# A third seven-product column set, block sums by accumulating transfers and four shared block buffers, in a decoder trunk on one core

## The chip, the core and the metric

The kernel runs on one NeuronCore of a Trainium2 chip. The metric is the device time of one execution in microseconds (us). A profile is one execution recorded instruction by instruction; engine names are those of the profile: PE (TensorE, matmuls; PEld is its weight load), DVE (VectorE), ACT (ScalarE), POOL (GpSimd), SP (SyncE, which issues most transfers).

## The reference, cut to what matters

Four layers on 256 rows of width 1024. Each layer is a half-step SwiGLU feed-forward network (FFN), a token mixer with memory attention, and another half-step FFN; every part is normalised before and after. So there are eight FFNs, and they hold most of the multiplications.

```python
def swiglu_ffn(x, w_gate_up, w_down):
    gate, up = jnp.split(x @ w_gate_up, 2, axis=-1)
    return (jax.nn.silu(gate) * up) @ w_down
...
x = x + 0.5 * rms_norm(swiglu_ffn(rms_norm(x, g[0]), ffn_w_gate_up[i, 0], ffn_w_down[i, 0]), g[1])
```

`w_gate_up` is 1024 x 5632 (gate and up of width 2816 each), `w_down` 2816 x 1024. All is float32.

## The kernel before, in words

**A product in three matmuls.** Each float32 operand is split into a high part `hi` (rounded to the fp32r type by ACT, L309) and the rest `lo` (DVE, L310), and a product is hi·hi + hi·lo + lo·hi (`mm3`, L334 to L336). So each unit of weights (128 partitions x 1024 columns, 512 KB) needs one ACT and one DVE operation before PE can use it.

**The ring of units.** `plan()` writes out the order in which PE takes units. `split_next` splits the next one into a ring of `RING` = 10 hi/lo pairs; `pump`, called from `slot` after each unit that PE has used, keeps the splits up to nine units ahead. Raw units come from HBM by SP's queue (`fetch`, L240) into three `raw` buffers.

**Column sets.** An FFN's 2816 gate and up columns are worked in six sets: sets 0 to 4 of 512 gate columns and the 512 up columns that go with them, set 5 of 256 and 256. For each set, the 256 rows (two halves, t = 0 and 1) are multiplied by gate and up, `silu` and the multiplication give T, T is transposed by PE (`turn_set`, L557) and split into `hh` and `hl`, and the rows of `w_down` that match (D units, 12 matmuls each, L684) are added into two accumulators. `FILL` says how many D units stand in which set; the last 8 stand at the end of the FFN.

**Normal sets and seven-product sets.** A normal set has 8 units and 96 matmuls (2 row halves x 8 chunks of the inner dimension x 3 parts x gate and up). In the sets of `SEVEN` (2 and 4) the product is seen as 2 x 2 blocks: row halves by inner halves of x, and inner halves by (gate, up) of the weights (b11, b12, b21, b22). Winograd's form of Strassen's method needs seven block products instead of eight: 14 units and 84 matmuls (`product`, L615). Its price is sums of blocks. Those of x are made once per FFN (`sums`, L599). Those of the weights are made in `operand`: for products 2, 3, 4 and 5 DVE adds one block to another before the split (L277; two halves each, so eight per set). Those of the results are made in `seven`: `snap` copies a PSUM buffer to SBUF (ACT, L623), and DVE adds (c11 L635, c22 L646, c12 L658).

In `seven`, three PSUM buffers a, b, c are taken at the start. Products 0, 3, 4 and 5 accumulate in a, 1 in b, 2 and 6 in c. There are four such buffers (`rot`), and the transposes of the set before, `turned(s - 1)`, stand after product 1 and take two. D units stand after product 3 (two) and product 4 (two).

**Block buffers.** The four weight blocks of a seven-product set are 8 KB per partition each. They borrow the buffers of tiles that are idle in an FFN: tags `rows` (normalised rows), `mgh` and `mgl` (memory and mixer outputs), and `q22` in the FFN's own pool. A block is loaded in two halves, in the order b11, b21, b12, b22, one half per call of `slot` in the set before.

**Order on the queues.** Each engine works its queue in order. The order is fixed when the program is built, from when operands and buffers are expected to be free; SP's transfers are thus often issued ahead of where they stand in the source, as soon as their buffer is released.

Of the kernel before, what the change touches and what calls it, by code (L numbers as in the profile page):

```python
# [53 lines left out]


SETS = 6
SEVEN = (2, 4)
FILL = {1: (2, 2), 3: (1, 1)}
QUADS = 8


def ffn_chunks(l, f):
    order = []
    nd = 0

    def fill(n):
        nonlocal nd, order
        order += [("D", l, f, nd + i) for i in range(n)]
        nd += n

    for s in range(SETS):
        if s in SEVEN:
            for ops, n in (((0, 1, 2, 3), 2), ((4,), 2), ((5, 6), 0)):
                order += [("S", l, f, s, op, h) for op in ops for h in range(2)]
                fill(n)
            continue
        for c, n in zip(("e",) if s == SETS - 1 else ("g", "u"), FILL.get(s, (0, 0))):
            order += [(c, l, f, s, i) for i in range(4)]
            fill(n)
    return order + [("D", l, f, j) for j in range(nd, NF)]  # L80
# [123 lines left out]
class Trunk:  # L204
    def __init__(self, ctx, tc, io):
        self.ctx, self.tc, self.nc, self.io = ctx, tc, tc.nc, io
        pool = lambda name, bufs=1, **kw: ctx.enter_context(tc.tile_pool(name=name, bufs=bufs, **kw))
        self.const = pool("const")
        self.wp = pool("wp")
        self.main = pool("main")  # L210
        self.small = pool("small", 4)
        self.ps = pool("ps", space=bass.MemoryType.PSUM)
        self.dram = pool("dram", space=bass.MemoryType.DRAM)
        self.plan = plan()
        self.offs = {}
# [11 lines left out]
        self.quad = None  # L227
        self.quad_loads = deque()

    def rot(self, *shape):  # L230
# [18 lines left out]
        self.raws.append((t, a * b))  # L249
        self.loaded += 1  # L250

    def new_quad(self, fp, l, f, s):
        self.quad = [None] * 4
        self.quad_pool = fp
        self.quad_set = (l, f, s)
        self.quad_loads = deque(quads(l, f, s))

    def load_quad(self):
        key = self.quad_loads.popleft()
        q, h = key[4:]  # L260
        if h == 0:
            pool, tag = ((self.main, "rows"), (self.main, "mgh"), (self.main, "mgl"), (self.quad_pool, "q22"))[q]
            self.quad[q] = pool.tile([P, 2, 1024], F32, tag=tag, name="quad")
        self.fetch(self.quad[q][:, h, :], key)

    def quads_for(self, key):
        if self.quad is None or self.quad_set != key[1:4]:
            return None
        return max(0, len(self.quad_loads) - (QUADS - (2 * min(key[4], 3) + key[5] + 1)))

    def can_split(self):
        key = self.plan[self.split_n]
        return key[0] != "S" or self.quads_for(key) == 0

    def operand(self, op, h):
        b11, b12, b21, b22 = (t if t is None else t[:, h, :] for t in self.quad)
        add = lambda x, y: self.nc.vector.tensor_tensor(out=x, in0=x, in1=y, op=ALU.add)  # L277
        if op == 2:
            add(b11, b12)
        elif op == 3:  # L280
            add(b11, b22)
        elif op == 4:
            add(b12, b22)
        elif op == 5:
            add(b21, b11)
        return (b11, b21, b11, b11, b12, b21, b22)[op]

    def split_next(self):
        key = self.plan[self.split_n]
        hi = self.wp.tile([P, 1024], F32R, tag="hi", name="hi", bufs=RING)  # L290
        lo = self.wp.tile([P, 1024], F32R, tag="lo", name="lo", bufs=RING)
        if key[0] == "S":
            for _ in range(self.quads_for(key)):
                self.load_quad()
            self.split(hi, lo, self.operand(*key[4:]))
# [60 lines left out]
    def ln_stages(self, st, t, ps, post_scale, post_eps, gpost, gpre):  # L356
# [9 lines left out]

        def rows():
            if st["rows"] is None:
                st["rows"] = self.main.tile([P, 2, D], F32, tag="rows", name="rows")
            return st["rows"][:, t, :]  # L370

        def s1():
# [30 lines left out]
                nc.scalar.activation(out=keep(t, k0 // 4), in_=ps, func=AF.Copy)  # L403

    def new_xt(self, a="xth", b="xtl"):
        return tuple(self.main.tile([P, KD, SEQ], F32R, tag=n, name=n) for n in (a, b))

    def boundary(self, ys, post, pre):
# [120 lines left out]
    def ffn(self, l, f, post_next, pre_next, last=False):  # L529
        nc, tc = self.nc, self.tc  # L530
        with tc.tile_pool(name=f"ffn{l}{f}", bufs=1, reuse_waits="tile") as fp:
# [61 lines left out]
            def sums():  # L593
# [10 lines left out]
                a11 = tuple(v[:, 0:4, 0:P] for v in xt)  # L604
                a12 = tuple(v[:, 4:8, 0:P] for v in xt)
                a22 = tuple(v[:, 4:8, P:] for v in xt)
                return a11, a12, S1, S2, S3, a22, S4

            def product(s, op, ps, fresh=False, after=None):
                for h in range(2):  # L610
# [15 lines left out]
            def seven(s):  # L626
                tt = nc.vector.tensor_tensor
                v = {}
                a, b, c = self.rot(), self.rot(), self.rot()
                T0, T1 = T[s]  # L630
                keep = lambda n: lambda: v.__setitem__(n, snap(a))
                product(s, 0, a, True, keep("P1"))

                def c11():
                    tt(out=v["P1"], in0=v["P1"], in1=b, op=ALU.add)  # L635
                    silu(T0, v["P1"])

                product(s, 1, b, True, c11)
                turned(s - 1)
                product(s, 2, c, True)  # L640
                product(s, 3, a, False, keep("U2"))
                fill(2)

                def c22():
                    v["U3"] = snap(a)
                    tt(out=v["U3"], in0=c, in1=v["U3"], op=ALU.subtract)  # L646

                product(s, 4, a, False, c22)
                fill(2)

                def c21():
                    silu(T1, a)
                    tt(out=T1, in0=T1, in1=v["U3"], op=ALU.mult)

                product(s, 5, a, False, c21)

                def c12():
                    tt(out=v["U2"], in0=c, in1=v["U2"], op=ALU.subtract)  # L658
                    tt(out=T0, in0=T0, in1=v["U2"], op=ALU.mult)

                product(s, 6, c, False, c12)

            first_set()
            left = sums()
# [36 lines left out]
            for s in range(1, SETS):  # L701
                T[s] = [tile_T(), tile_T()]
                if s + 1 in SEVEN:
                    self.new_quad(fp, l, f, s + 1)
# [59 lines left out]

    def mem_kv(self, l):
        nc = self.nc
        km = self.mp.tile([P, 2, SEQ], F32, name="km")
        vm = self.mp.tile([P, 2, SEQ], F32, name="vm")
        ps = self.rot().rearrange("p (a b) -> p a b", a=2)
        for c in range(2):  # L770
            self.cols_unit(ps[:, c, :], self.memg, self.take("K", l, c))
# [55 lines left out]
        return got[0]  # L827

    def q_mem(self, l, c0, xt):
        qm = self.mp.tile([P, 2, SEQ], F32, name="qm")  # L830
# [498 lines left out]
```

## Time and profile before

| | before |
|---|---|
| runs shown (3) | median 1902.22 us, 1894.52 to 1907.36 |
| the profiled execution | 1902.04 us, span 1900.2 us |
| granted TensorE clock | 0.999 of full speed |
| read from HBM | 359.95 MB, 190 GB/s over the span |
| the chain that ended last, by engine | PE 60%, DVE 17%, DMA 12%, ACT 5%, issue 4% |
| block sums on DVE (L277) | 128, 154.2 us |
| splits of blocks (L309 and L310) | 224 each, 232.7 us on ACT and 269.4 us on DVE |

The profile gives for each engine the time in which it was busy; for PE, instructions overlap, so that a busy PE can still be a PE that waits. In lists of groups a row is: line, engine, operation, output <- inputs by the program's tile names, shape, xcount | busy us in all, mean ns of one | idle us of the engine just before them, and what ended that idle time. In a timeline a row is: start in us, duration in us, engine and operation, count, and in brackets the idle time before it and its releaser. In lists of waits the numbers are us in total, times, and the longest. In lists of transfers the last number is the median time from issue to landing.

### The profile page before, as it was taken

To read this page: it belongs to the slowest core of one execution; us is meant where nothing else is said; L and a number is where in the kernel's file an instruction comes from. 1 tells how busy PE (TensorE), PEld (TensorE's weight loads), DVE (VectorE), ACT (ScalarE), POOL (GpSimd) and SP (SyncE) were. 2 spreads that over 40 slices of the span, in tenths; PEclk is the share of its full clock that TensorE was granted. 3 is DMA by queue.
4 is the path that set the end of the run, shared out by engine and by line. 5 is a ranking of instruction groups with operands and counts; after the bars stand their busy time and mean duration, and the time that the engine had idled before them with its cause. 6 is when DMAs were issued, how large, how long until landed. Compare 5 with 4: busy or idle time off the path is not lost.

```text
span 1900.2 us, 25015 instructions
## 1 busy us (share of the span) xinstructions
PE 1858.8 (98%) x9406; PEld 1550.4 (82%) x9406; DVE 1514.9 (80%) x1828; ACT 1085.9 (57%) x1469; POOL 59.8 (3%) x115
## 2 busy tenths in 40 slices
PE   7999999999999999999999999999999999999998
PEld 5888888787878897888888889888888878988886
DVE  6987888896879768889697966878877886878894
ACT  5655656564656545655565656555556555656562
POOL 0000100000000000000000000000000000100000
PEclk9999999999999999999999999999999999999999
DMA  8646747545663663754566357275476535747632
GB/s 295 235 167 200 233 156 266 205 140 176 233 222 115 199 203 111 266 198 145 180 231 233 112 185 238 102 246 184 151 229 227 189 127 183 243 156 244 220 105 86
DMA packets 103865, 362.65 MB, mean 191 GB/s; under 512 B 12084, under 2 KB 16576, under 8 KB 103616
## 3 DMA queue, kind: packets, MB, share of 16 engines
q1 hardware_dynamic: 103568, 359.47, 56.5%
q8 instruction: 74, 1.21, 0.3%
q0 software_dynamic: 176, 1.59, 0.2%
q14 instruction: 47, 0.39, 0.1%
HBM read 359.95 MB, written 1.06 MB: 190 GB/s over the span
## 4 chain that ended last, share of the span: by engine, by line
PE 60%; DVE 17%; DMA 12%; ACT 5%; issue 4%; POOL 1%; ACTq 0%; SPq 0%; DVEq 0%
PE acc L684 15%; DMA raw<-in_w 12%; PE rot L615 9%; PE rot L334 9%; PE rot L336 9%; PE rot L335 9%; DVE lo L310 9%; ACT hi L309 4%; DVE quad L277 3%; PE acc L944 3%; PE rot L557 1%; PE rot L399 1%; PE rot L848 1%; DVE x L378 1%; PE rot L880 1%
## 5 line engine op out<-in xcount | busy, mean ns | idle before, releaser
L310 DVE TENSOR_TENSOR lo<-raw,hi 128x1024 fp32r<-128x1024 f32 (+1 forms) x515 | 624.4, 1219 | 216.9 <-ACT hi L309 207.5
L309 ACT ACTIVATE hi<-raw 128x1024 fp32r<-128x1024 f32 (+1 forms) x515 | 542.1, 1055 | 397.0 <-DMA raw<-in_w 259.0
L334 PE MATMUL rot<-hi,xth 128*128 128x512 f32 (+3 forms) x1072 | 414.9, 387 | 2.5 <-ACT hi L309 1.6
L336 PE MATMUL rot<-hi,xtl 128*128 128x512 f32 (+3 forms) x1072 | 411.6, 384 | 1.2 <-DVE xtl L310 1.1
L335 PE MATMUL rot<-lo,xth 128*128 128x512 f32 (+3 forms) x1072 | 411.6, 384 | 0.0
L309 ACT ACTIVATE hi<-quad 128x1024 fp32r<-128x1024 f32 x224 | 232.7, 1056 | 156.5 <-DVE quad L277 83.4
L310 DVE TENSOR_TENSOR lo<-quad,hi 128x1024 fp32r<-128x1024 f32 x224 | 269.4, 1220 | 7.2 <-ACT hi L309 6.2
L334 PEld LDWEIGHTS rot<-hi,xth 128*128 128x128 f32 x1072 | 202.1, 189 | 41.4 <-ACT hi L309 2.1
L336 PEld LDWEIGHTS rot<-hi,xtl 128*128 128x128 f32 x1072 | 201.9, 188 | 41.3 <-DVE xtl L310 2.3
L335 PEld LDWEIGHTS rot<-lo,xth 128*128 128x128 f32 x1072 | 202.1, 189 | 38.2
L684 PE MATMUL acc<-lo,hh 128*128 128x512 f32 x640 | 198.9, 390 | 0.0
L684 PE MATMUL acc<-hi,hh 128*128 128x512 f32 x640 | 198.0, 390 | 0.0
L684 PE MATMUL acc<-hi,hl 128*128 128x512 f32 x640 | 197.2, 389 | 0.0
L277 DVE TENSOR_TENSOR quad<-quad 128x1024 f32<-128x1024 f32 x128 | 154.2, 1220 | 0.9
L684 PEld LDWEIGHTS acc<-hi,hl 128*128 128x128 f32 x640 | 120.1, 188 | 25.0 <-DVE hl L310 0.2
L684 PEld LDWEIGHTS acc<-lo,hh 128*128 128x128 f32 x640 | 120.2, 188 | 24.8
L684 PEld LDWEIGHTS acc<-hi,hh 128*128 128x128 f32 x640 | 119.5, 188 | 24.3
L615 PE MATMUL rot<-hi,sh 128*128 128x512 f32 x256 | 103.0, 402 | 6.8 <-DVE snap L635 6.8
L615 PE MATMUL rot<-lo,sh 128*128 128x512 f32 x256 | 100.0, 391 | 0.0
L615 PE MATMUL rot<-hi,sl 128*128 128x512 f32 x256 | 97.4, 390 | 0.0
L374 DVE TENSOR_TENSOR rows<-acc,gpost 128x1024 f32<-128x1024 f32 x24 | 29.3, 1222 | 74.9 <-ACT junk L373 74.8
L615 PE MATMUL rot<-hi,xtl 128*128 128x512 f32 x192 | 74.8, 389 | 0.0
(212 smaller groups left out, 2439.8 us busy)
## 6 DMA issues: line engine op xcount, KB each, us to landing
raw<-in_w SPq DMA_DIRECT2D x504, 512.0 KB, 4.3
quad<-in_w SPq DMA_DIRECT2D x128, 512.0 KB, 5.8
gpre<-in_norm_g SPq DMA_DIRECT2D x12, 512.0 KB, 5.1
gpost<-in_norm_g SPq DMA_DIRECT2D x12, 512.0 KB, 5.4
memraw<-in_mem_t SPq DMA_DIRECT2D x32, 128.0 KB, 3.2
raw<-in_w SPq DMA_DIRECT2D x8, 384.0 KB, 3.5
sw<-in_sw SPq DMA_DIRECT2D x2, 768.0 KB, 8.1
cb<-cd POOLq DMA_DIRECT2D x1, 1536.0 KB, 9.9
```

The costliest lines, as they stand in the source:

```text
L277: add = lambda x, y: self.nc.vector.tensor_tensor(out=x, in0=x, in1=y, op=ALU.add)
L309: self.nc.scalar.activation(out=hi, in_=src, func=AF.Copy)
L310: self.nc.vector.tensor_tensor(out=lo, in0=src, in1=hi.bitcast(F32), op=ALU.subtract)
L334: mm(out, a[0], b[0], start=start, stop=False)
L335: mm(out, a[0], b[1], start=False, stop=False)
L336: mm(out, a[1], b[0], start=False, stop=stop)
L374: nc.vector.tensor_tensor(out=rows(), in0=ps, in1=gpost, op=ALU.mult)
L378: nc.vector.scalar_tensor_tensor(out=x, in0=rows(), scalar=r, in1=x, op0=ALU.mult, op1=ALU.add)
L399: nc.tensor.transpose(ps[:, (k - k0) * P:(k - k0 + 1) * P], rows[:, k * P:(k + 1) * P], self.ident)
L615: nc.tensor.matmul(ps, a[i], w[j][:, kk, :], start=fresh and h == kk == i == j == 0, stop=h == kk == i == 1, skip_group_check=True)
L684: mm(ys[t][:, n * 512:(n + 1) * 512], x, y[:, 0, n * 512:(n + 1) * 512], start=(j == 0 and x is a[0] and y is w[0]), stop=(j == NF - 1 and ...
L944: self.nc.tensor.matmul(o["y"][t][:, h * 512:(h + 1) * 512], x, y[:, 0, h * 512:(h + 1) * 512], start=(j == 0 and x is a[0] and y is w[0]) ...
```

## The change

Sets 2, 3 and 4 now have seven products. The seven products are put in another order (the block sums are 11, 21, 11+12+22, 12+22, 11+12, 21+11+12+22, 22), so that two of the four weight sums are left to DVE (product 2's addition and product 4's subtraction, four operations per set with their halves), and two are done by transfers with accumulation issued on POOL's queue (`gather`): b22 into b12 as soon as both have landed, and the new b11 into b21 after product 2's sum. Product 2 and the later ones therefore need all four blocks of their set. In `seven`, c is taken after product 3; products 0, 2, 3 and 5 accumulate in a, 1 in b, 4 and 6 in c; D units stand after product 2 and after product 6 (`SFILL`: two and two in sets 2 and 4, one and one in set 3). The number of D units ahead of the end of the FFN, 14, is as before. The four block buffers become four buffers of one tag, `big`, shared by the blocks of all three sets, the normalised rows and the memory and mixer outputs. The small tiles km, vm and qm of the mixers move into the four `snap` buffers.

```diff
-SEVEN = (2, 4)
-FILL = {1: (2, 2), 3: (1, 1)}
-QUADS = 8
+SEVEN = (2, 3, 4)
+FILL = {1: (2, 2)}
+SFILL = {2: (2, 2), 3: (1, 1), 4: (2, 2)}
+SEVEN_OPS = ((0, 1, 2), (3, 4, 5, 6))
...
+    def big(self, *shape, dtype=F32):
+        return self.main.tile([P, *shape], dtype, tag="big", name="big", bufs=4)
...
         if h == 0:
-            pool, tag = ((self.main, "rows"), (self.main, "mgh"), (self.main, "mgl"), (self.quad_pool, "q22"))[q]
-            self.quad[q] = pool.tile([P, 2, 1024], F32, tag=tag, name="quad")
-        self.fetch(self.quad[q][:, h, :], key)
+            quad[q] = self.big(2, 1024)
+        self.fetch(quad[q][:, h, :], key)
+        if q == 3:
+            self.gather(quad[1][:, h, :], quad[3][:, h, :])
+
+    def gather(self, x, y):
+        self.nc.gpsimd.dma_start(out=x, in_=y, accum_op=ALU.add)
...
-        return max(0, len(self.quad_loads) - (QUADS - (2 * min(key[4], 3) + key[5] + 1)))
+        left = sum(k[1:4] == key[1:4] for k in self.quad_loads)
+        need = (2 * key[4] if key[4] < 2 else 6) + key[5] + 1
+        return max(0, need - (8 - left))
...
         if op == 2:
-            add(b11, b12)
-        elif op == 3:
-            add(b11, b22)
+            self.nc.vector.tensor_tensor(out=b11, in0=b11, in1=b12, op=ALU.add)
+            self.gather(b21, b11)
         elif op == 4:
-            add(b12, b22)
-        elif op == 5:
-            add(b21, b11)
-        return (b11, b21, b11, b11, b12, b21, b22)[op]
+            self.nc.vector.tensor_tensor(out=b11, in0=b11, in1=b22, op=ALU.subtract)
+        return (b11, b21, b11, b12, b11, b21, b22)[op]
...
-                return a11, a12, S1, S2, S3, a22, S4
+                return a11, a12, S2, S3, S1, a22, S4
...
-                a, b, c = self.rot(), self.rot(), self.rot()
+                a, b = self.rot(), self.rot()
...
                 product(s, 1, b, True, c11)
                 turned(s - 1)
-                product(s, 2, c, True)
-                product(s, 3, a, False, keep("U2"))
-                fill(2)
+                product(s, 2, a, False, keep("U2"))
+                fill(SFILL[s][0])
+                product(s, 3, a, False, keep("U3"))
+                c = self.rot()
 
                 def c22():
-                    v["U3"] = snap(a)
                     tt(out=v["U3"], in0=c, in1=v["U3"], op=ALU.subtract)
 
-                product(s, 4, a, False, c22)
-                fill(2)
+                product(s, 4, c, True, c22)
...
                 product(s, 6, c, False, c12)
+                fill(SFILL[s][1])
...
-        km = self.mp.tile([P, 2, SEQ], F32, name="km")
-        vm = self.mp.tile([P, 2, SEQ], F32, name="vm")
+        km = self.main.tile([P, 2, SEQ], F32, tag="snap", name="km", bufs=4)
+        vm = self.main.tile([P, 2, SEQ], F32, tag="snap", name="vm", bufs=4)
```

The tiles `rows` of a boundary and the pairs of `new_xt("mgh", "mgl")` are taken from `big` in the same way, and qm from `snap`.

More of the change, by code (lines that the diff above doesn't have):

```diff
@@ L72, in ffn_chunks @@
         if s in SEVEN:
-            for ops, n in (((0, 1, 2, 3), 2), ((4,), 2), ((5, 6), 0)):
+            for ops, n in zip(SEVEN_OPS, SFILL[s]):
                 order += [("S", l, f, s, op, h) for op in ops for h in range(2)]
@@ L226, in __init__ @@
         self.xf = {}
-        self.quad = None
+        self.quads = {}
         self.quad_loads = deque()
@@ L250, in load_next, with new_quad @@
         self.loaded += 1
[L252 to L256, printed above, removed]
+    def new_quad(self, l, f, s):
+        self.quads[l, f, s] = [None] * 4
+        self.quad_loads.extend(quads(l, f, s))
+    def big(self, *shape, dtype=F32):
+        return self.main.tile([P, *shape], dtype, tag="big", name="big", bufs=4)
     def load_quad(self):
         key = self.quad_loads.popleft()
+        quad = self.quads[key[1:4]]
         q, h = key[4:]
         if h == 0:
-            pool, tag = ((self.main, "rows"), (self.main, "mgh"), (self.main, "mgl"), (self.quad_pool, "q22"))[q]
-            self.quad[q] = pool.tile([P, 2, 1024], F32, tag=tag, name="quad")
-        self.fetch(self.quad[q][:, h, :], key)
+            quad[q] = self.big(2, 1024)
[4 more added lines that the diff above has]
+        self.nc.gpsimd.dma_start(out=x, in_=y, accum_op=ALU.add)
     def quads_for(self, key):
-        if self.quad is None or self.quad_set != key[1:4]:
+        if key[1:4] not in self.quads:
             return None
-        return max(0, len(self.quad_loads) - (QUADS - (2 * min(key[4], 3) + key[5] + 1)))
+        left = sum(k[1:4] == key[1:4] for k in self.quad_loads)
+        need = (2 * key[4] if key[4] < 2 else 6) + key[5] + 1
+        return max(0, need - (8 - left))
     def can_split(self):
@@ L273, in can_split, with operand @@
         return key[0] != "S" or self.quads_for(key) == 0
-    def operand(self, op, h):
-        b11, b12, b21, b22 = (t if t is None else t[:, h, :] for t in self.quad)
-        add = lambda x, y: self.nc.vector.tensor_tensor(out=x, in0=x, in1=y, op=ALU.add)
+    def operand(self, l, f, s, op, h):
+        b11, b12, b21, b22 = (t if t is None else t[:, h, :] for t in self.quads[l, f, s])
         if op == 2:
-            add(b11, b12)
-        elif op == 3:
-            add(b11, b22)
+            self.nc.vector.tensor_tensor(out=b11, in0=b11, in1=b12, op=ALU.add)
+            self.gather(b21, b11)
         elif op == 4:
-            add(b12, b22)
-        elif op == 5:
-            add(b21, b11)
-        return (b11, b21, b11, b11, b12, b21, b22)[op]
+            self.nc.vector.tensor_tensor(out=b11, in0=b11, in1=b22, op=ALU.subtract)
+        return (b11, b21, b11, b12, b11, b21, b22)[op]
     def split_next(self):
@@ L294, in split_next @@
                 self.load_quad()
-            self.split(hi, lo, self.operand(*key[4:]))
+            self.split(hi, lo, self.operand(*key[1:]))
         else:
@@ L368, in rows @@
             if st["rows"] is None:
-                st["rows"] = self.main.tile([P, 2, D], F32, tag="rows", name="rows")
+                st["rows"] = self.big(2, D)
             return st["rows"][:, t, :]
@@ L405, in new_xt @@
     def new_xt(self, a="xth", b="xtl"):
+        if a != "xth":
+            return tuple(self.big(KD, SEQ, dtype=F32R) for _ in range(2))
         return tuple(self.main.tile([P, KD, SEQ], F32R, tag=n, name=n) for n in (a, b))
@@ L703, in ffn @@
                 if s + 1 in SEVEN:
-                    self.new_quad(fp, l, f, s + 1)
+                    self.new_quad(l, f, s + 1)
                 if s in SEVEN:
@@ L829, in q_mem @@
     def q_mem(self, l, c0, xt):
-        qm = self.mp.tile([P, 2, SEQ], F32, name="qm")
+        qm = self.main.tile([P, 2, SEQ], F32, tag="snap", name="qm", bufs=4)
         ps = self.in_cols(l, c0, xt)
```

## The prediction

> **What bounds the kernel now.** First the page's busy times and DMA queues.
>
> ```profile
> span 1900.2 us, 25015 instructions
> PE 1858.8 (98%) x9406; PEld 1550.4 (82%) x9406; DVE 1514.9 (80%) x1828; ACT 1085.9 (57%) x1469; POOL 59.8 (3%) x115
> q1 hardware_dynamic: 103568, 359.47, 56.5%
> q0 software_dynamic: 176, 1.59, 0.2%
> ```
>
> PE is busy 98% of the span, but modelled ends overlap, so I check it by starts. Below is the timeline of PE at a seven-product set (FFN 1 of layer 0).
>
> ```profile
> 406.01 0.39 PE L615 MATMUL rot<-hi,xth 128*128 128x512 f32 x1
> ...
> 411.22 0.40 PE L615 MATMUL rot<-hi,xtl 128*128 128x512 f32 x1
> 411.45 1.04 PE L557 MATMUL rot<-ident,T 128*128 128x128 f32 x8
> 412.25 0.47 PE L615 MATMUL rot<-hi,sh 128*128 128x512 f32 x1
> ```
>
> The 24 matmuls of products 0 and 1 start from 406.01 to 411.22: 5.21/23 = 0.227 us apart, with no hole. So inside an FFN the end is set by the number of PE instructions, and a 128x512 matmul costs 0.227 us, not its 0.39 us. The eight transposes cost 412.25 - 411.45 = 0.80 us. Two D units are as dense (the next two rows, 152.38 - 146.94 = 5.44 us, 2.72 each).
>
> ```profile
> 146.94 0.62 PE L684 MATMUL acc<-hi,hh 128*128 128x512 f32 x2
> ...
> 152.38 0.39 PE L615 MATMUL rot<-hi,sh 128*128 128x512 f32 x1
> ```
>
> Now who is next. The table of busy time by stretches has sets 1 to 4 of that FFN as rows.
>
> ```profile
> core 0: us, PE busy (x) PEld busy (x) DVE busy (x) ACT busy (x) POOL busy (x), PEclk, DMA share, GB/s
> 316.74:344.04 27.30, 27.30 (x124) 22.61 (x122) 23.60 (x24) 14.36 (x17) 0.00 (x0) 1.00 0.37 122
> 344.04:376.95 32.91, 31.15 (x142) 25.53 (x140) 25.98 (x25) 20.29 (x23) 0.00 (x0) 1.00 0.76 271
> 376.95:406.01 29.06, 28.32 (x130) 23.27 (x128) 27.93 (x30) 14.57 (x16) 0.00 (x0) 1.00 0.26 91
> 406.01:437.01 31.00, 31.00 (x141) 25.54 (x140) 23.45 (x23) 20.18 (x23) 0.00 (x0) 1.00 0.72 227
> ```
>
> DVE is close behind: 27.93 of 29.06 us in set 3, where it prepares set 4 in advance. So PE is the bound with DVE as the second limit, and DMA has room on average (0.26 to 0.76).
>
> The one hole that these sets show again and again is this, from the timelines of PE and of DVE and the list of waits:
>
> ```profile
> 351.27 0.39 PE L615 MATMUL rot<-lo,sh 128*128 128x512 f32 x1
> 353.43 0.50 PE L615 MATMUL rot<-hi,sh 128*128 128x512 f32 x1 [1.76 <-DVE snap L635]
> 352.69 0.68 DVE L635 TENSOR_TENSOR snap<-snap,rot 128x512 f32<-128x512 f32 x1
> PEld rot L615 <- DVE snap L635: 12.5, 16, 2.2
> PEld rot L557 <- DVE T L659: 7.6, 7, 1.9
> PE rot L557 <- DVE T L659: 4.8, 6, 1.5
> ```
>
> Four PSUM buffers (rot) hold a, b and two transposes; a product that needs the fifth, c, waits until c11 on DVE (L635) has read b. It happens in all 16 sets, 12.5 us in total.
>
> **The change, part by part.**
>
> *PE.* Set 3 goes from 96 matmuls to 84 in each of 8 FFNs: 96 fewer at 0.227 = **-21.8 us**. It lies on the path, as the starts show.
>
> *Order of products and PSUM.* c is now taken after product 3, when b has long been read. The wait above goes: **-12.5 us**. c22 must now be done before product 6 with only product 5 (2.72 us) between, and its U3 copy is made a product earlier; c22's add takes 0.68 us like L635's. c12 now has a fill of one or two D (2.72 or 5.44 us) and two products before the next transposes, so of the 4.8 us of waits for T (L659) I count **-3** (bounds 0 and -4.8). Against that, the first D after product 2 needs hl of the set just transposed:
>
> ```profile
> 353.29 1.28 DVE L310 TENSOR_TENSOR hl<-rot,hh 128x512 fp32r<-128x512 f32 x2
> ```
>
> Product 2 would end 5.44 + 0.80 + 2.72 = 8.96 us after the set's start, and the first matmul that reads hl comes four later, at 9.87. Here the first hl ends at about 353.9, 9.9 us after the set's start at 344.04. It just about fits in this late case; I take **+3** for 24 sets, between 0 and the rate of the wait that it replaces (12.5 x 24/16 = 18.8).
>
> *DVE and ACT.* These rows from the list of groups price the work:
>
> ```profile
> L310 DVE TENSOR_TENSOR lo<-quad,hi 128x1024 fp32r<-128x1024 f32 x224 | 269.4, 1220 | 7.2 <-ACT hi L309 6.2
> L309 ACT ACTIVATE hi<-quad 128x1024 fp32r<-128x1024 f32 x224 | 232.7, 1056 | 156.5 <-DVE quad L277 83.4 <-PE rot L336 38.3 <-PE rot L615 15.7
> L277 DVE TENSOR_TENSOR quad<-quad 128x1024 f32<-128x1024 f32 x128 | 154.2, 1220 | 0.9
> L623 ACT ACTIVATE snap<-rot 128x512 f32<-128x512 f32 x48 | 28.4, 591 | 8.8 <-PE rot L615 8.8
> ```
>
> Block sums on DVE fall from 16 to 12 per FFN: -32 x 1.22 = -39.0 us. Set 3 splits 14 units instead of 8: +48 x 1.22 = +58.6. Three combining adds per new set: +24 x 0.68 = +16.3. DVE gains 36 us in all, ACT 48 x 1.06 + 24 x 0.59 = 65 us. Does this fit under PE? Back to back DVE is faster than its durations:
>
> ```profile
> 339.01 2.35 DVE L277 TENSOR_TENSOR quad<-quad 128x1024 f32<-128x1024 f32 x2
> 341.28 0.68 DVE L727 TENSOR_TENSOR T<-T,rot 128x512 f32<-128x512 f32 x1
> 341.87 1.22 DVE L310 TENSOR_TENSOR lo<-quad,hi 128x1024 fp32r<-128x1024 f32 x1
> ```
>
> That is (341.28 - 339.01)/2 = 1.135 us per 1024 columns and 0.59 per 512. Sets 2 and 4: 14 splits, 4 sums, 4 D splits (22 x 1.135) and 9 short operations (5.3) = 30.3 us against PE's 84 x 0.227 + 0.80 + 4 x 2.72 = 30.7. Set 3 with two D: 28.0 against 25.3. Over the three sets DVE falls 1.9 us behind, far less than its lead: of the three splits from 357.68 in the next rows the last, the final unit of its set, ends at 361.28, and PE uses it at 375.59, 14.3 us later. So DVE's work is hidden: **0**. At 1.22 per operation the lag would be 7.6 us, still under 14.3. ACT needs about 21 of set 3's 25.3: hidden too.
>
> ```profile
> 357.91 0.62 PE L684 MATMUL acc<-hi,hh 128*128 128x512 f32 x2
> 357.68 3.60 DVE L310 TENSOR_TENSOR lo<-quad,hi 128x1024 fp32r<-128x1024 f32 x3 [0.16 <-ACT hi L309]
> 375.59 0.39 PE L615 MATMUL rot<-hi,sh 128*128 128x512 f32 x1
> ```
>
> *Transfers.* 12 accumulating transfers of 512 KB per FFN, 96 in all, replace sums that DVE did in 1.22 us. No row shows one. The nearest, from the DMA issues (us to landing last):
>
> ```profile
> quad<-in_w SPq DMA_DIRECT2D x128, 512.0 KB, 5.8
> cd<-ct POOLq DMA_DIRECT2D x1, 12.0 KB, 3.3
> cb<-cd POOLq DMA_DIRECT2D x1, 1536.0 KB, 9.9
> ```
>
> POOL's queue needs 3.3 us for almost nothing, so G, the time of one accumulate, is at least that; 1.5 MB took 9.9 us, and an accumulate reads two blocks and writes one, 1.5 MB of traffic, so I take 9.9 as the upper end. By bytes read once, 512 KB comes at 3.3 + 6.6 x 500/1524 = 5.5 us. By bytes read twice it is 7.6. I take the middle, G = 6.6. [...]
>
> *Four shared buffers: the loop.* Until now set 4's blocks were fetched early, during set 2 (DMA at 0.76 there and 0.26 in set 3, in the table above). Now set s+1's last block can be fetched only when set s's last block (b22) has been split, and products 2 and later wait for the sum in that block. Positions from set 2's start: S6's second half follows S2's second half by ten units, the ring's length. In the rows above, the unit ten before was used up at 357.91 and the split ended at 361.28, 3.4 later. Now S2 ends at 8.96, so the split ends at 12.3. Fetch 5.8: 18.1. Gather G. From there DVE does two sums, ten splits, two subtractions, a D split and about six short operations up to S6 of set 3: 15 x 1.135 + 6 x 0.59 = 20.6, so 38.7 + G. Again 5.8 + G, then sum, hi and lo (1.22 + 1.06 + 1.22 = 3.5): S2 of set 4 is ready at 48.0 + 2G. PE wants it at 30.7 + 25.3 + 6.24 = 62.2. So it is in time for **G up to 7.1 us**; above that every us costs 2 us per FFN, 16 us in all. At 5.5 nothing, at 7.6 8 us, at 9.9 45 us. At 6.6 nothing, but with G spread over these I take **+4**. The second transfer of a set, into b21, has seven DVE operations (about 8 us) to hide under; above G = 8 its rest would add to the loop.
>
> *What moves besides.* Load bytes are the same. On SP the block fetches wait for buffers with D's loads behind them; three raw buffers and the nine-unit lead cover it, and without that cover a D would be late by a fetch, some 5 us per set. The POOL queue holds nothing else in these sets (0.00 busy in the table). Row, memory and output tiles share the four buffers, at most three at once in a mixer, and km, vm, qm use the snap buffers, idle there: 0; if one waited, about 1 us per mixer.
>
> **Sum.** The profiled execution took 1902.04 us (span 1900.2), beside a median of 1902.22 shown, so no correction. 1902.0 - 21.8 - 12.5 - 3 + 3 + 4 = **1871.7, say 1872 us**. Its own range: 1863 (no give-back) to 1883.
>
> **The rivals.**
>
> A, *the gather is late* (slower). The loop above is the mechanism, its place set 4's product 2 and its price 16 us per us of G over 7.1. What was gained is 34.3 + 3 - 3 = 34; it is given back where G = 7.1 + 34/16 = 9.2 us. At 9.9: 1902 - 34 + 45 = 1913. At 12, if the fetch traffic slows it (0.76 of the DMA engines were busy in set 2 already): 78 from the loop and some 4 us per FFN of b21's, 32 more, so 1978. For it: the block fetches that end the loop land in the same microseconds. Against it: DMA was at 0.26 in set 3, and fetches are now spread over three sets.
>
> B, *the wait moves* (same). A sum that waits for its gather stands in DVE's in-order queue; c11, c22 and hl behind it are late, and PE stalls at the D or at product 6 as often as it now does for c: 18.8 instead of my 3 in all, and no T gain: 1902 - 21.8 - 12.5 + 18.8 + 4 = 1890.5. For it: L635 above ran 3 us after its product ended, behind splits. Against it: DVE has fewer sums to do before product 2.
>
> C, *PE's saving does not show* because DVE is the bound. Then time would follow DVE's +36 us, and the lag in sets 2 to 4 would have to pass 14.3 us; at 1.9 to 7.6 it does not. If it did, 1902 + 36 = 1938.
>
> **Chances.** The forecast 0.55, B 0.20, A 0.20, C 0.05. One per cent (19 us; the three runs before lie between 1894.52 and 1907.36) is about what a measurement can tell. The forecast lies below 1883: faster 0.55. B lies within 1%: 0.20. A and C: A holds a stretch (G 8 to 9.8) that still ends within 1%, but I count A as slower: 0.25. The range runs from 1862 up to 1935: beyond it only A's far half and C, and what would be under 1862.
>
> **What would show it.** Right: 96 fewer matmuls with starts 0.227 us apart in set 3; waits for L635 gone; accumulate landings under 7 us; in set 4 product 2 without a hole. Wrong: landings of 9 us and more, DVE idle before the sum with the gather as releaser, holes of some us at set 4's product 2 in each FFN (A); PE waiting for hl or for c22 in every set (B); DVE without gaps and lead near zero from set 3 on (C). Landings well over 10 us, or sets 2 to 4 longer than 86.7 us, would make the forecast wrong.

## The result and the profile after

The changed kernel takes 1963.8 us (median of 4, 1960.8 to 1969.0) beside 1902.7 us for the kernel before on the same chip: a ratio of 1.033, interval 1.029 to 1.037. It is slower by 61 us, where 30 us faster was forecast. The profiled execution took 1964.9 us. Its page has these lines:

```profile
span 1963.1 us, 25368 instructions
...
PE 1868.0 (95%) x9310; PEld 1550.6 (79%) x9310; DVE 1543.8 (79%) x1868; ACT 1135.3 (58%) x1541; POOL 143.8 (7%) x211
...
q1 hardware_dynamic: 103568, 359.47, 53.8%
q0 software_dynamic: 14000, 51.92, 13.4%
...
big<-big POOLq DMA_DIRECT2D x96, 512.0 KB, 5.1
```

9406 - 9310 = 96 matmuls are gone, as promised, and the 96 accumulating transfers land 5.1 us after their issue (the median). VectorE is no busier in share than before. The loss is in holes of PE: adding up all that lies between the starts of matmuls beyond their normal spacing gives 84 us before and 168 us after, and -21.8 + 168 - 84 = +62. PE's list of waits names the holes, and VectorE's says what VectorE itself waits for:

```profile
PE rot L564 <- DVE T L726: 21.9, 15, 2.8
PE rot L622 <- ACT snap L630: 20.0, 8, 3.7
PE acc L691 <- ACT hh L314: 17.9, 10, 3.2
...
DVE big L287 <- DMA big<-big: 40.7, 24, 4.1
```

The wait for c (L635 before) has left the list. In its place stand T of set 5 at the FFN's end (L726), the copy of P1 that product 2 needs (L630), and hh. The table by stretches shows one FFN: sets 2, 3 and 4 and, within set 4, a hole and what follows it.

```profile
core 0: us, PE busy (x) PEld busy (x) DVE busy (x) ACT busy (x) POOL busy (x), PEclk, DMA share, GB/s
547.15:577.97 30.82, 30.82 (x142) 25.60 (x140) 24.61 (x26) 19.81 (x23) 3.48 (x4) 1.00 0.83 247
577.97:606.56 28.59, 25.78 (x117) 20.95 (x116) 24.69 (x26) 16.59 (x21) 1.72 (x2) 1.00 0.78 230
606.56:637.80 31.24, 27.99 (x121) 22.94 (x120) 29.44 (x32) 21.15 (x26) 1.72 (x2) 0.95 0.50 132
612.50:616.10 3.60, 0.54 (x5) 0.30 (x3) 3.60 (x4) 3.60 (x5) 0.00 (x0) 1.00 0.74 146
616.30:619.60 3.30, 3.30 (x8) 2.63 (x9) 3.30 (x4) 2.23 (x4) 0.00 (x0) 0.50 0.76 227
```

Set 2 is dense, set 3 has lost 3 us, set 4 holds a hole of 3.6 us (during it VectorE and ScalarE are busy all the time), and after it the granted clock is 0.50. From the timelines of VectorE, ScalarE and PE, that hole in order:

```profile
606.05 1.23 DVE L287 TENSOR_TENSOR big<-big 128x1024 f32<-128x1024 f32 x1 [3.41 <-DMA big<-big]
...
607.37 1.06 ACT L314 ACTIVATE hi<-big 128x1024 fp32r<-128x1024 f32 x1 [5.45 <-DVE big L287]
610.91 1.06 ACT L314 ACTIVATE hi<-big 128x1024 fp32r<-128x1024 f32 x1 [2.49 <-DVE big L287]
...
615.67 0.57 ACT L630 ACTIVATE snap<-rot 128x512 f32<-128x512 f32 x1
...
612.01 1.03 PE L564 MATMUL rot<-ident,T 128*128 128x128 f32 x8
616.29 0.80 PE L622 MATMUL rot<-hi,sh 128*128 128x512 f32 x1 [3.25 <-ACT snap L630]
616.89 0.63 PE L622 MATMUL rot<-lo,sh 128*128 128x512 f32 x1
617.31 0.63 PE L622 MATMUL rot<-hi,sl 128*128 128x512 f32 x1
```

VectorE waits for its transfer; ScalarE's splits wait for VectorE; the P1 copy, whose product of 12 matmuls began at 606.56 and was done at 609.3, stands behind them; and product 2, which now accumulates into the same buffer, waits for the copy. Then the matmuls start 0.42 us apart (617.31 - 616.89) instead of 0.227.

### The profile page after: what moved, and what is told of

It reads as the page before. It is cut to its first block, busy times and chain, and to the rows that moved or that the text cites. A ratio compares the mean times of both kernels' runs of the same rounds, so it can differ in the third digit from the quotient of the medians.

```text
span 1963.1 us, 25368 instructions
## 1 busy us (share of the span) xinstructions
PE 1868.0 (95%) x9310; PEld 1550.6 (79%) x9310; DVE 1543.8 (79%) x1868; ACT 1135.3 (58%) x1541; POOL 143.8 (7%) x211
## 3 DMA queue, kind: packets, MB, share of 16 engines
HBM read 359.95 MB, written 1.06 MB: 184 GB/s over the span
## 5 line engine op out<-in xcount | busy, mean ns | idle before, releaser
L315 DVE TENSOR_TENSOR lo<-raw,hi 128x1024 fp32r<-128x1024 f32 (+2 forms) x451 | 545.0, 1218 | 183.0 <-ACT hi L314 176.6
L314 ACT ACTIVATE hi<-raw 128x1024 fp32r<-128x1024 f32 (+2 forms) x451 | 471.9, 1053 | 330.0 <-DMA raw<-in_w 218.6
L314 ACT ACTIVATE hi<-big 128x1024 fp32r<-128x1024 f32 x336 | 344.1, 1054 | 177.0 <-DVE big L287 105.2
L315 DVE TENSOR_TENSOR lo<-big,hi 128x1024 fp32r<-128x1024 f32 x336 | 398.1, 1218 | 11.7 <-ACT hi L314 9.8
L339 PE MATMUL rot<-hi,xth 128*128 128x512 f32 (+3 forms) x816 | 314.7, 386 | 2.3 <-ACT hi L314 1.6
L341 PE MATMUL rot<-hi,xtl 128*128 128x512 f32 (+3 forms) x816 | 312.1, 383 | 1.1 <-DVE xtl L315 1.1
L340 PE MATMUL rot<-lo,xth 128*128 128x512 f32 (+3 forms) x816 | 312.1, 383 | 0.0
L691 PE MATMUL acc<-hi,hh 128*128 128x512 f32 x640 | 206.6, 405 | 17.9 <-ACT hh L314 17.9
L622 PE MATMUL rot<-hi,sl 128*128 128x512 f32 x384 | 152.3, 397 | 0.0
L271 POOL DMA_DIRECT2D big<-big x96 | 83.3, 867 | 839.2 <-DMA big<-in_w 282.7
L622 PE MATMUL rot<-hi,xth 128*128 128x512 f32 x288 | 112.0, 389 | 0.0
```

The lines of the kernel that those rows point to most:

```text
L271: self.nc.gpsimd.dma_start(out=x, in_=y, accum_op=ALU.add)
L314: self.nc.scalar.activation(out=hi, in_=src, func=AF.Copy)
L315: self.nc.vector.tensor_tensor(out=lo, in0=src, in1=hi.bitcast(F32), op=ALU.subtract)
L339: mm(out, a[0], b[0], start=start, stop=False)
L340: mm(out, a[0], b[1], start=False, stop=False)
L341: mm(out, a[1], b[0], start=False, stop=stop)
```

## The experiments

The theory at first was **W**: a sum that waits for its transfer stands at the head of VectorE's queue, and copies queue up behind it. Its rivals were **O**, the new order of products and D units leaves too little slack, and **D**, three sets in a row are too dense for VectorE. The runs were made on several chips, each with its own runs of the kernel before, so kernels are compared by ratio; 1% is 19 us. The expectations are in times, most of them worked out from runs of another chip; where the ratio says something else than the time, it is named.

**1. Take the transfers away** (their 96 sums are left out).

```
 def gather(self, x, y):
-    self.nc.gpsimd.dma_start(out=x, in_=y, accum_op=ALU.add)
+    pass
```

> Leaves out the 96 accumulating transfers, and with them the sums b12+b22 and b21+b11; all else as in the changed kernel. Theory W (a sum that waits for its transfer stands at the head of DVE's and ACT's in-order queues, and the P1 copy and hh behind it come late for PE): the waits go, about 60 to 75 us less than the changed kernel, 1885 to 1905 us. Theory O (the new order of products and D units leaves P1's copy and hh too little time, whatever the transfers do): 1945 us and more. Theory D (three seven-product sets in a row leave DVE and ACT no slack): 1940 us and more, since DVE's and ACT's work is unchanged.

1904.3 us, ratio 0.998 (0.996 to 1.000): 66 us back, in W's range. The waits for P1 and hh are gone, as W says. But 0.998 is not the gain that the matmuls promise: the tail's wait is as long as ever (the row below). Nor is it the transfers' traffic on the DMA engines that makes loads of weight units late: without transfers they land in 4.4 us in the median, with them in 4.3.

```profile
PE rot L564 <- DVE T L726: 26.0, 16, 3.5
```

**2. The same sums on VectorE.** `gather` becomes `self.nc.vector.tensor_tensor(out=x, in0=x, in1=y, op=ALU.add)`, called just ahead of the split.

> Makes the 96 transferred sums on DVE in operand (b12+b22 before product 2's sum, b21+b11 after it), so that nothing waits for a transfer between blocks but DVE has 96 x 1.22 = 117 us more. Theory W: the head-of-line waits go, DVE's lag over sets 2 to 4 becomes some 15 us, as much as the lead: 1895 to 1930 us. Theory D: DVE is denser, so slower than the changed kernel, 1980 us and more. Theory O: 1955 us or more.

1922.9 us, ratio 1.008 (1.005 to 1.011). VectorE is busy 1645.5 us (86%) instead of 1543.8, and yet the kernel is 47 us faster than with transfers: it is not VectorE's load that makes the changed kernel slow. W's range is met, D's and O's are not.

**3 and 4. The order.** Two sets instead of three, all else as changed; then, with three sets, the first fill after product 3 instead of product 2 (hh gets a product more).

```
-SEVEN = (2, 3, 4)
-FILL = {1: (2, 2)}
-SFILL = {2: (2, 2), 3: (1, 1), 4: (2, 2)}
+SEVEN = (2, 4)
+FILL = {1: (2, 2), 3: (1, 1)}
+SFILL = {2: (2, 2), 4: (2, 2)}
```

> Seven products in sets 2 and 4 only, with set 3 normal and the D units as in the kernel before; transfers, order of products and shared buffers as in the changed kernel. Theory W: set 4's blocks and their transfers come during the normal set, so hardly a sum waits: 1885 to 1900 us (the wait for c gone). Theory D: the same, 1885 to 1905. Theory O: every one of the 16 sets keeps its holes of 2 to 3 us, 1920 to 1945 us.

1935.4 us, ratio 1.016 (1.013 to 1.019): in O's range, W's and D's missed.

> The first D units of a seven-product set stand after product 3 again instead of after product 2; all else as changed. Theory O: the holes before the D units (hh) go and with them their half-clock stretches, 25 to 40 us less: 1925 to 1940 us. Theory W: hh's hole goes but the P1 copy's and T's stay and the last unit of set s is split later, so 1945 to 1965 us. Theory D: no change, within 10 us of 1964.

1967.4 us, ratio 1.032 (1.029 to 1.035): no change. The wait for hh fell from 17.9 to 11.3 us and that for P1 rose from 20.0 to 26.1. O missed here; W's range (just, by the ratio) and D's are met.

**5. Hold the sums back**, four half-products behind the transfer's issue: `can_split` also asks `self.ticks >= self.due.get(key[1:], 0)`, with `due` set at the transfer and `ticks` counted in `slot`.

> All three sets and all transfers stay; a unit whose sum waits for a transfer is given to ScalarE and VectorE only four half-products after the transfer was issued, so that the copies for P1 and hh stand ahead of it in both queues. W (the sum that waits at the head of an in-order queue is what costs): the waits for the P1 copy (20.0 us) and for hh (17.9 + 22.1 us on the two rows) fall to less than half, 1920 to 1945 us; less than without transfers, since in set 4 the block itself comes late. Rival T (the transfer costs by its traffic or by being late as such): the units become late instead, PE waits for lo or hi, and the time stays at 1955 to 1975 us.

1957.8 us, ratio 1.031 (1.028 to 1.035): W's simple form fails, and the time lies in rival T's range, although PE waits for no late unit as T would have it. PE still waits 21.3 us for the P1 copy, and VectorE still 37.6 us for transfers at the sums of L287. So the hold did not take away the wait that it was to take away: four half-products are 5.4 us, and a first transfer of a set takes 7.35 us (the median in the changed kernel's trace). Whether a longer hold would do was not tried.

**6. Two sets, sums on VectorE:** edits 2 and 3 together, the kernel before with the new order alone.

> Two sets as before, the new order of products and fills and the shared buffers, but all block sums on VectorE (128 as before). This is the kernel before with the order alone. W: the loss of the two-set run (1935 us) came from the transfers; without them 1895 to 1912 us. O (the order of products, D units and fetches leaves too little slack): 1925 to 1940 us, with the waits for hh where they were (15.9 us). R (a new one: three load buffers, each held for some 7 us from the load's issue to the end of lo, give one weight unit per 2.3 us, and a long row of weight units without block units between runs dry): two such rows per FFN, 1910 to 1930 us.

1895.7 us, ratio 0.998 (0.997 to 1.000). O is out: the new order costs nothing. R, which this expectation names for the first time, missed too (1910 us and more). The order gains little either: the wait for c has left the list, and yet the kernel is only 3 us faster. Beside the same sums on VectorE the 64 transfers of run 3 cost 1.0156 - 0.9982 = 1.7%, 33 us.

**7 and 8. The tail.** The third theory, **R** (the load buffers run dry), came from ScalarE's timeline in the run without transfers. These are the last splits of an FFN, all of weight units:

```profile
625.41 1.06 ACT L314 ACTIVATE hi<-raw 128x1024 fp32r<-128x1024 f32 x1 [0.41 <-DMA raw<-in_w]
628.06 1.06 ACT L314 ACTIVATE hi<-raw 128x1024 fp32r<-128x1024 f32 x1 [1.58 <-DMA raw<-in_w]
630.66 1.06 ACT L314 ACTIVATE hi<-raw 128x1024 fp32r<-128x1024 f32 x1 [1.55 <-DMA raw<-in_w]
...
640.23 1.06 ACT L314 ACTIVATE hi<-raw 128x1024 fp32r<-128x1024 f32 x1 [1.87 <-DMA raw<-in_w]
```

From 625.41 to 640.23 there are seven such splits, 14.8/6 = 2.5 us apart, and six of them wait for their load. A load buffer is taken from the load's issue until lo is done: about 4.3 us to landing, 1.06 for hi, 1.22 for lo, 6.6 us, so by estimate three buffers give a unit per 2.2 us at best. The last eight D units want one per 1.36 us (6 matmuls of 0.227 us for each row half).

```
-RING = 10
-RAW = 3
+RING = 9
+RAW = 5
```

> Three sets, all sums on VectorE (1922.9 us), five load buffers instead of three, paid for with a ring of nine instead of ten. R: the waits of ScalarE for raw (227 us) fall below 100, the losses of the FFN's tail (waits for T of set 5, 14.8 us, and the half-clock stretches behind them, 12 us) fall to less than half, 1900 to 1912 us. D (VectorE at 86% is the bound): no change, 1918 to 1928 us.

1904.5 us, ratio 1.003 (1.002 to 1.004), from 1.008: 10 us. No wait for T of set 5 is left, and ScalarE's waits for loads fall from 227 to 81 us. By its waits R holds; by the ratio the time is 1914 us on the chip of run 2, 2 us over R's range.

> Three sets, all sums on VectorE (1922.9 us); the second fill stands between products 4 and 5 as before, and the transposes of set 5 come two D units later (2.7 us more slack for T). R: weight units and block units alternate again, the tail's waits for T fall to less than a third, 1895 to 1912 us. D: VectorE is the bound, the holes move elsewhere, 1915 to 1925 us.

1907.9 us, ratio 1.005 (1.004 to 1.007): at most 6 us of the same loss (the intervals overlap; by the ratio it is 1918 us on the chip of run 2, in D's range), by giving T more time instead of loading earlier (`SEVEN_OPS = ((0, 1, 2), (3, 4), (5, 6))`, and `turned(5)` at `nd + 4`).

**9 to 11. Buffers with transfers, and neither.** Five shared buffers (`bufs=5` in `big`, RING 9); five load buffers with transfers (RAW 5, RING 9); five load buffers without transfers.

> The changed kernel with its transfers, five shared buffers instead of four, paid for with a ring of nine instead of ten. L (the loop through the four buffers: the next set's last block is fetched only when this set's is split, so its transfer lands when its sum already stands at the head of VectorE's queue): the waits of VectorE for transfers (40.7 + 7.4 us) fall below 15, the waits for the P1 copy and hh with them, 1915 to 1940 us. Rival T (the transfers cost by their traffic, or each by its own 5 us whatever the buffers): waits stay, 1950 to 1970 us.

1942.5 us, ratio 1.024 (1.020 to 1.029): 16 us, VectorE's wait at L287 from 40.7 to 25.7. The time lies between the two ranges, and VectorE's wait did not fall below 15 us as L asks. The loop through four buffers is a part, and not the main one.

> The changed kernel with its transfers and four shared buffers, but five load buffers instead of three and a ring of nine. R (three load buffers run dry in a row of weight units): with the sums on VectorE this gave 10 us; here the tail's waits for T (21.9 us) and part of the half-clock stretches go, 1940 to 1955 us, and the waits for the P1 copy (20.0 us) stay. If R alone were the cause: 1905 to 1915 us. If R plays no part with transfers: 1958 to 1970 us.

1912.8 us, ratio 1.008 (1.005 to 1.011): 48 us, near what was expected if R alone were the cause. It is not alone: of the three waits in PE's list the one for P1 is left, which leaving out the transfers took away in run 1, and hl comes in:

```profile
PE rot L622 <- ACT snap L630: 22.9, 15, 2.8
...
PE acc L691 <- DVE hl L315: 6.9, 7, 2.1
```

> No transfers and none of their 96 sums (left out: b12 plus b22 and b21 plus b11, so seven products are formed from unsummed blocks), five load buffers, a ring of nine: what three sets are worth once nothing waits. By the 96 matmuls (21.8 us) and the waits for c (12.5 us) the kernel before less 34 us, 1866 to 1876 us beside its 1900; if the rest of the new order costs something of its own, 1880 to 1895 us.

1862.8 us, ratio 0.981 (0.979 to 0.984), a little under the range. Its page:

```profile
span 1861.2 us, 25028 instructions
...
PE 1833.1 (98%) x9310; PEld 1533.9 (82%) x9310; DVE 1536.5 (83%) x1868; ACT 1144.7 (62%) x1543; POOL 65.8 (4%) x115
```

VectorE and ScalarE do all that the changed kernel makes them do (1543.8 and 1135.3 us there), and the holes of PE are 68 us, fewer than before. D is out.

**12. The sums on GpSimd**, five load buffers: `self.nc.gpsimd.tensor_tensor(out=x, in0=x, in1=y, op=ALU.add)`.

> Three sets with the 96 sums on GpSimd instead of transfers, five load buffers, a ring of nine: VectorE has the load of the changed kernel, and a sum has no transfer to wait for. W: if GpSimd takes under 3 us for 128x1024 and leaves VectorE alone, 1875 to 1895 us. If it takes 5 us or more, or slows VectorE's 1.22 us operations, the sum is late as with transfers: 1915 to 1960 us.

1992.0 us, ratio 1.049 (1.047 to 1.052), outside both ranges. The list of groups has the price, and what it does to VectorE:

```profile
L271 POOL TENSOR_TENSOR big<-big 128x1024 f32<-128x1024 f32 x96 | 283.6, 2963 | 705.5 <-DMA big<-in_w 457.5 <-DVE lo L315 86.8 <-DVE big L287 62.7
...
L315 DVE TENSOR_TENSOR lo<-big,hi 128x1024 fp32r<-128x1024 f32 x336 | 505.3, 1534 | 22.5 <-ACT hi L314 21.1
L287 DVE TENSOR_TENSOR big<-big 128x1024 f32<-128x1024 f32 x48 | 86.2, 1798 | 11.3 <-POOL big L271 9.9
```

A sum takes 2.96 us there, and VectorE's splits and sums of blocks, 1.22 us each in run 10, take 1.53 and 1.80 us.

**13 and 14. Which transfer?** With five load buffers, only the second by transfer (b11 into b21), the first sum on VectorE; and the mirror.

> Five load buffers, a ring of nine (1912.8 us with both transfers, 1862.8 without any and without their sums). The first sum (b22 into b12) on VectorE, only the second (b11 into b21) by transfer: VectorE has 48 operations of 1.22 us more than with both. If the first transfer is what costs: half of the 41 us that the 96 sums cost on VectorE stays (1904.5 against 1862.8), 1878 to 1890 us. If the second costs as much: 1900 to 1912 us.

1886.4 us, ratio 0.990 (0.987 to 0.993).

> The mirror: the first sum by transfer, the second (b11 into b21) on VectorE, five load buffers, a ring of nine. If the first transfer is what costs: 1912 to 1935 us (its 50 us and VectorE's 48 operations more). If the second costs as much: 1900 to 1912 us.

1916.4 us, ratio 1.006 (1.004 to 1.008). The time lies in the first range, but by the ratio it is 1909 us on the chip that the ranges came from, in the second; so the four kernels have to be compared. Beside the second transfer, making the first sum by transfer too costs 34 us (run 10, 1.008, against run 13, 0.990); beside the first, the second costs 4 (run 10 against run 14), within the noise. The first transfer is the one that costs. Against both sums on VectorE (run 7, 1.003) the second one gains 25 us as a transfer, and the first loses 5, within the noise. So the two don't add up: the second's gain shows only where the first is not a transfer. The DMA issues say how they differ (the last number is the median from issue to landing); the first row is from the run with the second transfer, the next from its mirror, and the third from the mirror's list of VectorE's waits:

```profile
big<-big POOLq DMA_DIRECT2D x48, 512.0 KB, 4.4
```

```profile
big<-big POOLq DMA_DIRECT2D x48, 512.0 KB, 7.0
```

```profile
DVE big L287 <- DMA big<-big: 56.2, 30, 7.2
```

**15. Is it SyncE's queue?** The block fetches go to GpSimd's queue, three load buffers, no transfers: `self.fetch(quad[q][:, h, :], key, self.nc.gpsimd)`.

> No transfers and none of their 96 sums (left out: b12 plus b22 and b21 plus b11), three load buffers, a ring of ten, as in the first run (1904 us); the block fetches are issued by GpSimd's queue instead of SyncE's. S (the loads stand behind block fetches that wait for a buffer): the tail's waits for T (26.0 us) go, 1862 to 1880 us, as with five load buffers (1862.8). R (three buffers are too few for a row of 14 weight units): 1895 to 1910 us.

1946.0 us, ratio 1.020 (1.017 to 1.023), outside both. Two things happen. PE's waits at the boundaries (L404) go from 15 to 39.9 us. There VectorE's operation on the rows (L390) stands behind splits whose loads are late, as in these rows of ScalarE and VectorE:

```profile
478.90 1.06 ACT L314 ACTIVATE hi<-raw 128x1024 fp32r<-128x1024 f32 x1 [5.47 <-DMA raw<-in_w]
479.99 1.23 DVE L315 TENSOR_TENSOR lo<-raw,hi 128x1024 fp32r<-128x1024 f32 x1 [5.60 <-ACT hi L314]
481.13 1.28 DVE L390 SCALAR_TENSOR_TENSOR big<-x,r,gpre 128x1024 f32<-128x1024 f32 x1
```

And the tail's wait stays, at 20.3 us (26.0 in run 1), with ScalarE's for loads at 229 us (200 in run 1). So S fails on its own number; the time itself tells nothing about the queue.

**16. Fill and turn moved as in run 8**, on run 13.

> The second transfer alone, five load buffers, a ring of nine, the second fill between products 4 and 5, the transposes of set 5 two D units later. If the runs before are read rightly (first transfer costs, load buffers cost, fill and turn were worth 15 us where the loads were short): 1872 to 1892 us, under both kernels. If fill and turn only helped where loads were short, the same as without them, within 6 us of the run above.

1889.8 us, ratio 0.991 (0.988 to 0.994): the same as run 13. If moving them helps at all, it is only where loads are short. (The 15 us in the expectation compared times of two chips; by ratio it was 6.)

**17. The kernel before with five load buffers.**

> The kernel before (two sets, sums on VectorE) with five load buffers and a ring of nine and nothing else. If the change makes the need: within 1% of the kernel before, 1895 to 1910 us. If three load buffers were short there too: 1870 to 1890 us, and the gain of the version with the second transfer alone would be the buffers', not the three sets'.

1883.8 us, ratio 0.989 (0.986 to 0.991). Three load buffers were already too few before the change. ScalarE's list of waits has it in one row, for the kernel before, for it with five load buffers, and for the changed kernel with five:

```profile
ACT hi L309 <- DMA raw<-in_w: 259.0, 226, 3.7
```

```profile
ACT hi L309 <- DMA raw<-in_w: 21.7, 30, 2.7
```

```profile
ACT hi L314 <- DMA raw<-in_w: 72.4, 71, 4.2
```

And in this run PE's list has no wait for L635 (the 12.5 us of the prediction) and none for T, with the old order of products.

**18. Two D units from set 1 to set 3**, on run 13. In that run VectorE was full from the middle of set 2 into set 4 (the columns of the table are those above):

```profile
540.00:570.00 30.00, 29.83 (x135) 24.24 (x134) 29.48 (x31) 19.58 (x25) 1.73 (x2) 1.00 0.58 178
570.00:600.00 30.00, 29.93 (x137) 24.49 (x135) 29.52 (x32) 19.44 (x26) 1.72 (x2) 1.00 0.52 158
```

```
-FILL = {1: (2, 2)}
-SFILL = {2: (2, 2), 3: (1, 1), 4: (2, 2)}
+FILL = {1: (1, 1)}
+SFILL = {2: (2, 2), 3: (2, 2), 4: (2, 2)}
```

> The kernel with the second transfer alone and five load buffers (1886.4 us, 0.9898 of the kernel before), with two of the four D units of set 1 moved to set 3. If VectorE's load in sets 2 and 3 is what holds it: the holes of 91.5 - 68 = 23 us go in part, 1866 to 1882 us, under the kernel before with five load buffers (0.9888, 1882.7 us on the clock of that run). If set 1, now shorter, starts set 2 with less lead: no change or up to 10 us worse, 1884 to 1896 us.

1872.9 us, ratio 0.984 (0.982 to 0.987), the fastest kernel that computes everything: 30 us under the kernel before, 9 us under it with five load buffers (the two intervals just touch).

## Why the prediction was wrong

The ratios to the kernel before, set out by load buffers:

| | three load buffers | five |
|---|---|---|
| kernel before | 1 | 0.989 |
| changed | 1.033 | 1.008 |
| changed, no transfers and none of their sums | 0.998 | 0.981 |
| changed, their sums on VectorE | 1.008 | 1.003 |
| changed, second transfer only | | 0.990 |

**Two steps failed.** The larger is the transfers' term, +4 us with +3 for hl: the first transfer of a set was to stay hidden as long as it took less than 7.1 us, and only units of weights were followed to see whether they would be late. With five load buffers the transfers and what they carry cost 1.0079 - 0.9813 = 2.7%, 51 us (with three 66 us, run 1); 34 us of it are the first transfer's, since without that one the cost is 0.9898 - 0.9813, 16 us, 48 sums on VectorE included. What was late was the copy of P1, which I had not priced: product 2 had written c and now writes on into a, so it needs that copy one product sooner.

The other is a sentence that carried no term: "three raw buffers and the nine-unit lead cover it, and without that cover a D would be late by a fetch, some 5 us per set". They did not cover even the old kernel, whose ScalarE waited 259 us for loads. I took such waits for slack, since PE was 98% busy, although DMA held 12% of the chain that ended last, in the table ahead of the prediction. The changed kernel needs the lead more: by the column of five, load buffers are worth 21 us before and 48 us after. That is 26 us of the 62.

Forecast and result lie 93 us apart by the ratios (-30 and +62.6). Of these the transfers are 44, the load buffers 26, and 23 are the terms for PE, c and T: -37.3 forecast, -14 measured (run 11 against run 17). Another order of taking things away shares them out otherwise, as the 66 us with three load buffers show.

**Rival B had the mechanism and the wrong size.** It said "A sum that waits for its gather stands in DVE's in-order queue; c11, c22 and hl behind it are late", at 18.8 us, and did not name the copy. The rows of set 4 above show the chain, and leaving out the transfers takes the wait for P1 away (run 1). That the sum's place in the queue is what counts is not shown by a run of its own: the hold of four half-products did not remove the wait (run 5).

Point by point:

- *PE, -21.8 us.* Right, within the noise. Between the kernel before with five load buffers and the changed one without sums the spans differ by 1882.2 - 1861.2 = 21.0 us (14 us by the ratios, whose intervals leave some 6 us on either side).
- *The wait for c, -12.5, and for T, -3.* The wait for c is gone, and the new order alone takes it away (run 6). But there it is worth 3 us by the ratio and not 15. And with five load buffers the old order has neither wait (run 17): VectorE was late with c11 where loads were late. Most of what was counted as the change's gain was to be had from the load buffers.
- *hl, +3.* With three load buffers it was hh, at 17.9 us. With five hh is gone and hl is at 6.9: the term was near, and the loads came on top.
- *VectorE's +36 us and ScalarE's +65 us, hidden: 0.* Right, as run 11 shows, where loads are early. (The lag at 1.22 us per operation comes to 7.3 us rather than 7.6, which changes nothing.) The lead of 14.3 us that I read was that of block units in one set; weight units at the end of an FFN have none.
- *Transfers, G = 6.6 us.* 5.1 for all; 4.4 for the second and 7.0 for the first, each measured alone. In the changed kernel's own trace the two kinds have medians of 4.44 and 7.35 us, with 11.6 at most. The second lies below even the 5.5 of bytes read once, so the 7.6 by two reads, which the middle was taken from, is shown by no run; the first stands at the 7.1 us up to which the forecast's loop was to hide it. Rival A's loop is real: five shared buffers give 16 us. But it is not A's sum that decides in the changed kernel, where PE's list has no wait for a unit of a seven-product set. (In run 14 it has one, 19.9 us for lo.)
- *C, VectorE as the bound.* Out, by runs 2 and 11. It seems to decide how much of the third set can be kept: with five load buffers and all sums on VectorE, three sets (run 7, 1.003) lose to two (run 17, 0.989), and run 18 gained by giving set 3 two more D units, which take PE 2.72 us each and VectorE about 1.2.
- *Not in the prediction:* the half clock, below.

Left open: why the first transfer takes 7.0 us and the second 4.4. The changed kernel's own trace, where they take 7.35 and 4.44 us, shows what goes with it. During the second transfers the packets of the other queues fill 0.01 of the DMA engines' time in the mean; during the first ones they fill 0.37, and 0.46 during the 34 of the 48 that take 6.5 us or more. With each of the first ones 2.5 loads of weight units overlap in the mean, and 0.5 block fetches. That this traffic makes the transfer slow is likely, but no run moves it without moving something else.

## What to carry to other kernels

Look up what an engine "off the path" waits for before trusting its share of slack: 259 us of ScalarE's waiting for loads stood behind waits that the list put down to VectorE, and two more load buffers, with a ring of nine, gave 1.1% with no other change. Price a buffer by its whole hold time (issue, landing, last reader) against the densest row of units that will pass through it, not by the mean. And move a sum to a transfer only where work that needs nothing from it stands between the two: with the other sum on VectorE the second sum gained 25 us that way, and the first, needed at once, gained nothing.

## What the runs showed of the hardware

- A hole in PE's work can cost more than its length. With many of the holes of 2 to 4 us, or of two shorter ones in a row, the granted clock goes to 0.50 for 3.4 us, three times for 6.8: the changed kernel has 15 such stretches in the clock's records (one of them, of 7.4 us, at the end, where the matmuls are done), 65.5 us in all. In the other 14 start 131 matmuls, 0.43 us apart in the median and not 0.227, so that by estimate some 26 us of its lost time lie in them. The kernel before has one such stretch, at the end; its granted clock is 0.999 in the mean and run 11's too, that of the changed kernel 0.984. Not every hole does it: after those of 2.6, 2.9 and 3.0 us that end at 118, 147 and 590 us the clock stays at 1.00, and after the shorter one of 2.1 us that ends at 397 us it is 0.50, so the length of a hole does not decide alone. What else decides is not shown.
- With the 96 sums on GpSimd (run 12) VectorE's operations on blocks take longer than in run 10, where the sums are transfers: the splits (L315) 1.53 us for 1.22, the sums at L287 1.80 for 1.22, the subtractions at L290 1.51 for 1.22. The splits of weight units go from 1.22 to 1.27 in the mean, and the combining operations of 128x512 stay at 0.68. Why they take longer is not shown.
- An accumulating transfer of 512 KB between SBUF buffers takes 4.4 us from issue to landing as the second of a set (run 13) and 7.0 us as the first (run 14). In the changed kernel's trace it is 4.44 us where the other queues fill 0.01 of the DMA engines' time and 7.35 where they fill 0.37. GpSimd needs 0.87 us to issue one:

```profile
L271 POOL DMA_DIRECT2D big<-big x96 | 83.3, 867 | 839.2 <-DMA big<-in_w 282.7 <-DVE lo L315 249.3 <-DVE big L287 83.6
```
